# A norm five ticks later, later loads of mixed values, and weight splits in halves, in a one-core decoder layer

## The chip, the cores and the metric

The kernel runs on one core of a Trainium2 chip, as one launch. The metric is device time in microseconds (us); a kernel's time is the median of its runs. The profile shows one execution of the same program: which instruction ran on which engine, when, and what it waited for. The engines are named as in the profile: PE multiplies matrices (PEld is its weight load), DVE works on vectors, ACT evaluates functions and copies, POOL starts the adding transfers here, and SP starts the other transfers, one after the other.

## What is computed

One layer of a decoder trunk, for 2048 tokens of 1024 values. The part that matters here is the output projection and the norms around it:

```
mix = concatenate(gated DeltaNet output, HGRN2 output)       # 2048 x 1024
mix_out = mix @ w_out
h = x + rms_norm(mix_out, post_mix_norm)
u = rms_norm(h, pre_mlp_norm) @ w_mlp_up
y = square(relu(u)) @ w_mlp_down
h = h + rms_norm(y, post_mlp_norm)
e = rms_norm(p @ w_ple_proj, ple_norm)
h = h + e * sigmoid(h @ w_ple_gate)
rms_norm(x, w) = x * rsqrt(mean(x * x) + eps) * w
```

Ahead of it stand the input projection and the two mixers, which are chunked recurrences over the tokens. All is in 32-bit floats.

## The kernel before

Values are kept transposed: 128 of the 1024 features on the partitions, 512 tokens (a quarter) along the free axis. So a quarter of the activations is eight tiles of 128 x 512, and an output tile of `mix_out` is one tile of 128 x 512 made from eight tiles of mixed values. Each operand is split into a high part (ACT, a rounding copy) and a low part (DVE, value minus high part), and each product takes three matmuls (high by high, high by low, low by high). An output tile of `mix_out` is therefore 24 matmuls.

**The order of the work.** PE's instructions run in the order in which the program is written. For ACT, DVE and, in this stage, SP, a planner sets the order: it goes by the order in which instructions are written and by its own idea of when each could start. At run time each engine keeps that order strictly. To place the work beside the matmuls, the program has an agenda: `tick()` moves a clock on by one and issues the next step of every generator that is due. In the output projection `mm` calls `tick()` before every eighth matmul, so an output tile is three ticks. `later(gen, offsets)` puts the steps of a generator at these offsets from the current clock; `at(t, gen, offsets)` does so from a given clock.

**Two parts of the projection.** The last head of the last quarter still has a long tail of small dependent matmuls. The first seven output tiles (quarter 0, features 0 to 6) are computed between these (`early_outs`, lines 983 to 1010), eight matmuls to a tick. Then the main loop over `order` (lines 1384 to 1444) computes the other 25 tiles, 600 matmuls, in the order of `OUT_ORDER`: quarter 0's last tile, eight of quarter 1, then quarters 2 and 3 mixed. Below, "matmul 232" is the 232nd of these 600, counted from 0; the clock is 417 before the first, so the tick `c` comes before matmul 8 x (c - 417).

**The weights.** A block of `w_out` (128 x 1024 values) is fetched by `stage_out` into one of two buffers and split by `ready_out` into one of three. `OUT_ORDER` makes 19 such blocks. Blocks 0 to 7 are split in the tail, 8 to 18 in the main loop.

**The mixed values.** `mix_operands(q)` fetches and splits one of eight tiles at each step: a transfer of 256 KB, an ACT copy (line 225) and a DVE subtraction (line 226). Quarters 2 and 3 are placed by `later` at lines 1382 and 1383.

**The norms.** When a quarter of `mix_out` is done, `normed` runs (line 1435): `rstd_steps` splits the sum of squares into `hl` (first step), sums it over the partitions by two matmuls with a tile of ones and makes the reciprocal root on ACT and DVE (second step; tiles `nrm_o`, `r_o`). `residual_by_dma` then scales one of eight tiles a step (DVE, line 1235), adds the input `x` to it by an adding transfer started by POOL (line 1236), and five steps later squares the sum (ACT, line 241), adds it to a running total `acc_h` (DVE, line 242) and stores the tile (SP, line 1239, `h1d`). Last comes `rstd_steps` again on `acc_h`, two steps: the split `hl_h`, and the matmuls `nrm_h` with the chain that makes `rn`. `OUT_STEPS` holds the 17 offsets for quarter 0, `OUT_LAST` those for quarter 1. The tile `hl` has one buffer for all norms. Quarters 2 and 3 only get their `r_o` here (line 1440).

**What follows from the norms.** Once quarter 0's `rn` is issued, the next tile's start places `early_operands` (eight steps; each fetches a tile of `h1d`, scales it and splits it, tiles `be` and `t`). Once quarter 1's is issued, whatever is left of these runs at once and `rest_operands` follows. These tiles and the split blocks `w_u` feed the up projection, which begins after matmul 599.

Of the kernel before, what the change touches and what calls it, by code (L numbers as in the profile page):

```python
# [11 lines left out]
F32R = mybir.dt.float32r  # L12
# [8 lines left out]
P = 128  # L21
T = 2048
D = 1024
KD = D // P
# [22 lines left out]
OUT_ORDER = ("00 01 02 03 04 05 06 07 17 16 15 12 13 14 10 11 20 21 30 22 31 23 32 24 33 34 25 26 27 35 36 37")  # L47
SHARE = 6
TOGETHER = ((1, 7), (1, 6))
OUT_STEPS = (1, 5) + tuple(range(7, 20)) + (20, 26)  # L50
OUT_LAST = (1, 4) + tuple(range(5, 18)) + (19, 23)
MLP_STEPS = (1, 5) + tuple(range(7, 25, 2))
AMID_STEPS = (1, 5) + tuple(range(12, 39, 3))
# [43 lines left out]
def trunk(ctx, tc, x, xT, pT, vecs, w_in, w_ab, gdn_a_log, gdn_dt_bias, w_out, w_up, w_down,  # L97
          w_ple, w_gate, consts, out):
    nc = tc.nc
    V, S, G, PE = nc.vector, nc.scalar, nc.gpsimd, nc.tensor  # L100
# [4 lines left out]
    wp = wctx.enter_context(tc.tile_pool(name="wp", bufs=3, side="right"))  # L105
# [8 lines left out]
    def bank(name, pool=None):  # L114
        return (pool or pm).tile([P, QT], F32, tag="ps", name=name)

    def blk(c):
        return slice(c * P, (c + 1) * P)
# [51 lines left out]
    def split(t, eng, raw):  # L170

        S.activation(t[:, 0], raw, AF.Copy)  # L172
        eng.tensor_tensor(t[:, 1], raw, t[:, 0], ALU.subtract)  # L173
# [45 lines left out]
    def plain(t):  # L219

        return t[:, 1].bitcast(F32)

    def split_in_place(t):

        S.activation(t[:, 0], plain(t), AF.Copy)  # L225
        V.tensor_tensor(t[:, 1], plain(t), t[:, 0], ALU.subtract)  # L226
# [99 lines left out]
    def next_pool():  # L326
        turn[0] += 1
        return ra if (turn[0] - 1) % 28 < 10 else second[0]
# [3 lines left out]
    def mix_operands(q):  # L332
        xin[q] = []
        for k in range(KD):
            t = next_pool().tile([P, 2, QT], F32R, tag="ring", name=f"mixT{q}_{k}")
            nc.sync.dma_start(plain(t), mixd[q][k])
            split_in_place(t)
            xin[q].append(t)
            yield
# [11 lines left out]
    staged_out, ready = {}, {}  # L351

    def ready_at(n):
        return 0 if n < 3 else sorted(last_use[:n])[n - 3] + 1

    def stage_at(n):
        return 0 if n < 4 else ready_at(n - 2) + 1

    def stage_out(n):
        staged_out[n] = wp.tile([P, KD, P], F32, tag="raw", name=f"raw_out{n}", bufs=2)  # L360
        nc.sync.dma_start(staged_out[n], w_out[tile_of[n]])

    def ready_out(n):
        ready[n] = wp.tile([P, 2, KD, P], F32R, tag="whl", name=f"w_out{n}")
        split(ready[n], V, staged_out.pop(n))

    clock, agenda = [0], {}

# [81 lines left out]
    with mixers as mctx:  # L450
# [504 lines left out]
        def at(t, gen, offsets):  # L955
            for o in offsets:
                agenda.setdefault(t + o, []).append(gen)

        def call(t, fn):
            def once():  # L960
                fn()
                yield
            at(t, once(), (0,))
# [17 lines left out]
        last, end = t + LAST, SPT * len(works)  # L981
# [1 line left out]
        for n, o in enumerate((-12, -8, -4, 0, 4)):  # L983
            call(end + o, partial(stage_out, n))
        for n, o in enumerate((-6, -1, 3)):
            call(end + o, partial(ready_out, n))
        finished, held_y, square_sums = [], [], {q: None for q in range(NQ)}

        def early_outs():

            for j, (q, d) in enumerate(order):
                for n in range(3, len(tile_of)):
                    if ready_at(n) == j:
                        ready_out(n)
                for n in range(5, len(tile_of)):
                    if stage_at(n) == j:
                        stage_out(n)
                ps, w = bank(f"mmo_{q}_{d}"), ready[load_of[j]]
                for i in range(3 * KD):
                    k, term = i // 3, i % 3  # L1000
                    PE.matmul(ps, w[:, term // 2, k, :], xin[q][k][:, term % 2, :], start=i == 0, stop=i == 3 * KD - 1)  # L1001
                    if i % 4 == 3 and i + 1 < 3 * KD:
                        yield
                        while i > KD and held_y:
                            nc.sync.dma_start(*held_y.pop())
                y = m2.tile([P, QT], F32, tag="ld", name=f"yo{q}_{d}", bufs=2)
                S.activation(y, ps, AF.Copy)
                square_sums[q] = squares(square_sums[q], ps, d, f"o{q}")
                finished.append(j)
                held_y.append((yod[q][d], y))  # L1010
                yield
# [129 lines left out]
    def later(gen, offsets):  # L1141
        for o in offsets:
            agenda.setdefault(clock[0] + o, []).append(gen)
# [21 lines left out]
    def ytile(name):  # L1165
        return f2.tile([P, QT], F32, tag="y", name=name, bufs=16)
# [103 lines left out]
    def run(gen):  # L1270
        for _ in gen:
            pass
# [95 lines left out]
    def two_blocks(*them):  # L1368

        w = wp.tile([P, 2, KD, P], F32R, tag="whl", name=f"w_u{them[0][0]}")  # L1370
        halves = [w[:, :, : KD // 2], w[:, :, KD // 2 :]]
        for t, it in zip(halves, them):
            if it:
                u_block(it[0], t, it[1])
        return halves[1]

    pair[0] = True
    early = None
    made, held = {q: [None] * KD for q in range(NQ)}, {}
    mix1 = mix_operands(1)  # L1380
    run(mix1)
    later(mix_operands(2), range(5, 21, 2))
    later(mix_operands(3), range(12, 28, 2))
    for j, (q, d) in enumerate(order):
        if j in finished:
            made[q][d] = ytile(f"yo{q}_{d}")
            nc.sync.dma_start(made[q][d], yod[q][d])
            continue
        for n in range(2, len(tile_of)):
            if ready_at(n) == j:  # L1390
                ready_out(n)
        for n in range(3, len(tile_of)):
            if stage_at(n) == j:
                stage_out(n)
        if j == len(order) - 5:
            u_raw = [wp.tile([P, 2, QT], F32, tag="raw", name=f"u_raw{i}", bufs=2) for i in range(2)]
            a1, a2 = w_up[0], w_up[FF // P // 2]
            for t, i, src in ((u_raw[0], 0, a1[:, : KD // 2]), (u_raw[1], 1, a1[:, KD // 2 :]),
                              (u_raw[0], 1, a2[:, : KD // 2]), (u_raw[1], 0, a2[:, KD // 2 :])):
                nc.sync.dma_start(t[:, i].rearrange("p (k n) -> p k n", n=P), src)  # L1400
        if j == len(order) - 2:
            two_blocks(("11", u_raw[0][:, 0]), ("12", u_raw[1][:, 1]))
        if j == len(order) - 1:
            (a11, a21), (s1, s4) = ((t[:, 0], t[:, 1]) for t in u_raw)
            b22 = two_blocks(("22", s1), None)
            V.tensor_tensor(s1, s1, a21, ALU.add)
            V.tensor_tensor(a21, a11, a21, ALU.subtract)
            V.tensor_tensor(a11, s1, a11, ALU.subtract)
            V.tensor_tensor(s4, s4, a11, ALU.subtract)
            u_block("3", b22, a21)  # L1410
            later(prep, range(3 * KD // 2))
        if early is None and h1_r[0] is not None:
            early = early_operands()
            later(early, range(0, 2 * KD, 2))
        if prep is None and h1_r[1] is not None:
            run(early)
            prep = rest_operands(h1_r[1])
            later(prep, range(3 * KD // 2))
        if j in held:
            ps = held.pop(j)  # L1420
        elif order[j] == TOGETHER[0]:
            held = {j + i: bank(f"mmo_{q}_{d}_{i}", pp) for i in range(len(TOGETHER))}
            sides = [columns(ready[load_of[i]]) for i in held]
            for k in range(KD):
                for i, w in zip(held, sides):
                    product(held[i], w[k : k + 1], xin[q][k : k + 1], k == 0, k == KD - 1)
            ps = held.pop(j)
        else:
            ps = bank(f"mmo_{q}_{d}", pp)
            product(ps, columns(ready[load_of[j]]), xin[q])  # L1430
        y = ytile(f"yo{q}_{d}") if q < 2 else tp.tile([P, QT], F32, tag="stg", name=f"yo{q}_{d}")
        S.activation(y, ps, AF.Copy)
        acc = square_sums[q] = squares(square_sums[q], ps, d, f"o{q}")
        made[q][d] = y
        if q >= 2:
            nc.sync.dma_start(yod[q][d], y)
        if all(of != q for of, _ in order[j + 1 :]) and q < 2:
            later(normed(q, made[q], acc, lambda d, q=q: xT[blk(d), tok(q)], R_POSTMIX, h1d[q], "o", "h"),
                  OUT_LAST if q else OUT_STEPS)
        elif all(of != q for of, _ in order[j + 1 :]):  # L1440
            later(rstd_steps(acc, 1.0 / D, EPS, f"o{q}", row_of(o_r, q), po, wait=True),
                  OUT_STEPS[:2] + (9,) if q == 2 else (12, 20, 24))
    u_block("2", two_blocks(("1", s1), None), a11)
    u_block("4", wp.tile([P, 2, KD // 2, P], F32R, tag="raw", name="w_u4", bufs=2), s4)
    run(prep)
# [468 lines left out]
```

## Time and profile before

| | us |
|---|---|
| median of 3 runs | 2713.89 (2713.32 to 2715.02) |
| the profiled execution's own time | 2702.87 |
| its span, first to last instruction | 2701.1 |
| PE busy | 2652.0 (98%) |
| DVE busy | 2031.1 (75%) |
| ACT busy | 1458.9 (54%) |
| POOL busy | 137.0 (5%) |
| tail with the first seven output tiles | about 1061.7 to 1121.4 |
| main loop of the output projection | 1121.4 to 1271.0 |

A row of the timeline gives an instruction's start, its duration, engine, line, operation, and output and input tiles; in brackets the idle time of the engine just before it and what ended that. Consecutive like instructions are merged into one row with a count. A row of the waits reads: who waited, for what, total us, times, longest. PE's matmuls overlap in the pipeline, so one is listed with 0.39 us while in a long row they follow one another at less than that.

### The profile page before, as it was taken

Reading aid. Unit: us, or ns where it says so; the run is one execution under the profiler, and the core shown is the slowest. Engines: PE = TensorE matmul, PEld = TensorE weight load, DVE = VectorE, ACT = ScalarE, POOL = GpSimd, SP = SyncE. Lnnn points to the kernel's source line nnn. Section 1 sums busy time; section 2 is a strip of 40 time slices with the busy share of each in tenths; the row PEclk is TensorE's granted clock in tenths of the full one; section 3 lists DMA queues with packets and bytes.
Section 4 is the critical chain, followed back from the end, with each engine's and each line's share of the span. In section 5 each row is a group of like instructions: output and inputs, shape, how many; then the busy total and the mean of one; then the engine's idle time right before and its main releaser. Section 6 shows DMA issues by size and latency. Waiting matters only on the chain.

```text
span 2701.1 us, 38432 instructions
## 1 busy us (share of the span) xinstructions
PE 2652.0 (98%) x12745; PEld 2210.0 (82%) x12745; DVE 2031.1 (75%) x4200; ACT 1458.9 (54%) x2935; POOL 137.0 (5%) x147
## 2 busy tenths in 40 slices
PE   8999999999999999999999999999999999999999
PEld 6788888888888887878888878888888888888887
DVE  7778878787778777578989867768877765468775
ACT  7665655465446445566556555554555555565431
POOL 0000000000000000020000000001000001101000
PEclk9999999999999999999999999999999999999999
DMA  8777777667666665584656466666544465577663
GB/s 278 275 242 247 239 250 248 224 222 249 209 211 219 211 212 187 181 224 153 210 205 213 172 223 218 210 201 236 191 160 145 165 225 185 201 249 247 216 215 125
DMA packets 267766, 573.51 MB, mean 212 GB/s; under 512 B 55578, under 2 KB 60152, under 8 KB 250416
## 3 DMA queue, kind: packets, MB, share of 16 engines
q1 hardware_dynamic: 265264, 566.86, 61.9%
q0 software_dynamic: 2304, 4.20, 0.9%
q8 instruction: 101, 1.65, 0.3%
q14 instruction: 97, 0.79, 0.1%
HBM read 410.57 MB, written 160.37 MB: 211 GB/s over the span
## 4 chain that ended last, share of the span: by engine, by line
PE 50%; issue 4%; DVE 3%; DMA 3%; ACT 2%; POOL 1%; SPq 0%; DVEq 0%; ACTq 0%; POOLq 0%
PE u L1150 22%; PE d L1150 19%; PE mmg L1150 6%; DMA dr<-in_w_down_dram 1%; PE mme L199 1%; PE mmo L1150 1%; PE mmo L1001 0%; POOL acc_y L242 0%; DMA h1d<-yo 0%; DMA sys_g<-ud_g 0%; DMA yo<-in_xT_dram 0%; DVE w_out L173 0%; DMA rd_g<-m_g 0%; DMA db<-hid 0%; DVE b L1306 0%
## 5 line engine op out<-in xcount | busy, mean ns | idle before, releaser
L1118 PE MATMUL mm<-xt,w 128*128 128x512 f32 x3072 | 783.9, 400 | 1.9 <-ACT zt_zg L592 1.3
L1118 PEld LDWEIGHTS mm<-xt,w 128*128 128x128 f32 x3072 | 553.4, 189 | 102.7 <-ACT zt_zg L592 1.7
L1150 PE MATMUL d<-db,da 128*128 128x512 f32 x2688 | 614.5, 389 | 2.0 <-ACT db L225 1.5
L1150 PEld LDWEIGHTS d<-db,da 128*128 128x128 f32 x2688 | 504.4, 188 | 108.4 <-ACT db L225 2.3
L1150 PE MATMUL u<-t,wu 128*128 128x512 f32 x2604 | 591.3, 389 | 0.0
L1150 PEld LDWEIGHTS u<-t,wu 128*128 128x128 f32 x2604 | 488.8, 188 | 101.5
L226 DVE TENSOR_TENSOR db<-db 128x512 fp32r<-128x512 f32 x224 | 161.1, 719 | 51.6 <-ACT db L225 50.6
L1537 DVE TENSOR_TENSOR u<-u,u 128x512 f32<-128x512 f32 x224 | 150.4, 683 | 57.3 <-PE u L1150 55.9
L1150 PE MATMUL mmg<-h2T,wg 128*128 128x512 f32 (+1 forms) x792 | 174.8, 383 | 0.0
L225 ACT ACTIVATE db<-db 128x512 fp32r<-128x512 f32 x224 | 140.9, 629 | 59.4 <-DMA db<-hid 55.4
L1580 ACT ACTIVATE u<-u 128x512 f32<-128x512 f32 x128 | 80.8, 631 | 164.3 <-DVE u L1537 163.6
L1150 PEld LDWEIGHTS mmg<-h2T,wg 128*128 128x128 f32 x792 | 145.6, 188 | 29.1
L173 DVE TENSOR_TENSOR da<-da 128x512 fp32r<-128x512 f32 x128 | 94.7, 740 | 77.6 <-ACT da L172 77.3
L1150 PE MATMUL mmo<-mixT,w_out 128*128 128x512 f32 x600 | 139.2, 393 | 0.3 <-DVE w_out L173 0.3
L172 ACT ACTIVATE da<-da 128x512 fp32r<-128x512 f32 x128 | 80.5, 629 | 108.8 <-DMA da<-sumd 82.0
L1150 PEld LDWEIGHTS mmo<-mixT,w_out 128*128 128x128 f32 x600 | 114.0, 190 | 24.5 <-DVE w_out L173 0.8
L173 DVE TENSOR_TENSOR da<-dr,da 128x512 fp32r<-128x512 f32 x96 | 68.9, 718 | 43.5 <-ACT da L172 41.8
L172 ACT ACTIVATE wu<-a 128x512 fp32r<-128x512 f32 x124 | 75.1, 623 | 44.6 <-DMA a<-in_w_up_dram 40.8
L713 DVE TENSOR_TENSOR pr_g<-xs_g,sys_g 128x16 f32<-128x16 f32 (+14 forms) x240 | 94.5, 394 | 5.7
L173 DVE TENSOR_TENSOR wu<-a,wu 128x512 fp32r<-128x512 f32 x124 | 85.7, 693 | 10.4 <-ACT wu L172 10.3
L1581 ACT ACTIVATE u<-u 128x512 f32<-128x512 f32 x128 | 80.5, 629 | 3.1
L172 ACT ACTIVATE da<-dr 128x512 fp32r<-128x512 f32 x96 | 60.5, 631 | 33.2 <-DMA dr<-in_w_down_dram 28.6
(390 smaller groups left out, 3821.3 us busy)
## 6 DMA issues: line engine op xcount, KB each, us to landing
w<-cache_in SPq DMA_DIRECT2D x96, 1024.0 KB
db<-hid SPq DMA_DIRECT2D x224, 256.0 KB
cache_in<-w SPq DMA_DIRECT2D x32, 1024.0 KB
hid<-u SPq DMA_DIRECT2D x128, 256.0 KB
da<-sumd SPq DMA_DIRECT2D x128, 256.0 KB
a<-in_w_up_dram SPq DMA_DIRECT2D x124, 256.0 KB
hid<-ht SPq DMA_DIRECT2D x96, 256.0 KB
dr<-in_w_down_dram SPq DMA_DIRECT2D x96, 256.0 KB
```

The costliest lines, as they stand in the source:

```text
L172: S.activation(t[:, 0], raw, AF.Copy)
L173: eng.tensor_tensor(t[:, 1], raw, t[:, 0], ALU.subtract)
L199: PE.matmul(ps, a, b, start=i == 0, stop=i == n - 1)
L225: S.activation(t[:, 0], plain(t), AF.Copy)
L226: V.tensor_tensor(t[:, 1], plain(t), t[:, 0], ALU.subtract)
L713: V.tensor_tensor(pr[:, :, :, 0:i], xs[:, None, :, 0:i].broadcast_to([P, 2, GC, i]), sys[:, 0:i, i : i + 2].rearrange("p j two -> p two j" ...
L1118: PE.matmul(ps, *terms[i], start=i == 0, stop=i == nt - 1)
L1150: PE.matmul(ps, a, b, start=start, stop=stop)
L1537: V.tensor_tensor(c[new], c[old], ps, ALU.add)
L1580: S.activation(c[k], c[k], AF.Relu)
L1581: S.activation(c[k], c[k], AF.Square)
```

## The change

Five things, all in or near the output projection:

- The last two offsets of `OUT_STEPS` go from 20 and 26 to 29 and 31: quarter 0's `hl_h` is split nine ticks later, and its norm (`nrm_h`, `rn`) follows five ticks later.
- `mix_operands` of quarters 2 and 3 starts three ticks later (8 and 15 instead of 5 and 12), with the same spacing.
- `early_operands` gets six places, two ticks apart, instead of eight; what is left of it runs when quarter 1's `rn` has been issued.
- Quarter 2's `r_o` is made at the offsets 8, 13 and 17 instead of 1, 5 and 9.
- The `w_out` blocks that are made ready in the tail (0 to 7) are split by a new generator in two halves, a tick apart, placed on the agenda.

```diff
-OUT_STEPS = (1, 5) + tuple(range(7, 20)) + (20, 26)
+OUT_STEPS = (1, 5) + tuple(range(7, 20)) + (29, 31)
...
+    def ready_halves(n):
+        ready[n] = wp.tile([P, 2, KD, P], F32R, tag="whl", name=f"w_out{n}")
+        raw = staged_out.pop(n)
+        for sl in (slice(0, KD // 2), slice(KD // 2, KD)):
+            split(ready[n][:, :, sl], V, raw[:, sl])
+            yield
...
         for n, o in enumerate((-6, -1, 3)):
-            call(end + o, partial(ready_out, n))
+            at(end + o, ready_halves(n), (0, 1))
...
                     if ready_at(n) == j:
-                        ready_out(n)
+                        at(clock[0], ready_halves(n), (0, 1))
...
-    later(mix_operands(2), range(5, 21, 2))
-    later(mix_operands(3), range(12, 28, 2))
+    later(mix_operands(2), range(8, 24, 2))
+    later(mix_operands(3), range(15, 31, 2))
...
             early = early_operands()
-            later(early, range(0, 2 * KD, 2))
+            later(early, range(0, 12, 2))
...
             later(rstd_steps(acc, 1.0 / D, EPS, f"o{q}", row_of(o_r, q), po, wait=True),
-                  OUT_STEPS[:2] + (9,) if q == 2 else (12, 20, 24))
+                  (8, 13, 17) if q == 2 else (12, 20, 24))
```

## The prediction, made before the result was known

> **What bounds the kernel now.** I read the page first (where PE loses time), then the waits of PE in the tail and in the main loop, then PE's timeline around the longest wait, and last the timelines of ACT, DVE and SP at that place.
>
> ```profile
> span 2701.1 us, 38432 instructions
> PE 2652.0 (98%) x12745; PEld 2210.0 (82%) x12745; DVE 2031.1 (75%) x4200; ACT 1458.9 (54%) x2935; POOL 137.0 (5%) x147
> ```
>
> PE is the bound; only its idle or slow time can be won. The waits of PE, tail first, then from 1121 us on:
>
> ```profile
> PE at_h L868 <- ACT keys_h L873: 2.1, 1, 2.1
> PE psb_g L784 <- DVE r_g L781: 1.4, 2, 0.9
> ...
> PE nrm_h L1181 <- ACT hl_h L172: 5.7, 1, 5.7
> PE u L1150 <- DVE w_u L173: 0.4, 1, 0.4
> ...
> PE u L1150 <- ACT w_u L172: 0.3, 1, 0.3
> ```
>
> The 5.7 us belong to quarter 0's second norm. PE's timeline, two rows of the tail and then there:
>
> ```profile
> 1075.93 0.71 PE L868 MATMUL at_h<-qk_h,keys_h 128*128 128x128 f32 x4 [2.05 <-ACT keys_h L873]
> 1076.40 1.17 PE L1001 MATMUL mmo<-mixT,w_out 128*128 128x512 f32 x4
> ...
> 1167.77 8.91 PE L1150 MATMUL mmo<-mixT,w_out 128*128 128x512 f32 x38 [0.33 <-DVE w_out L173]
> 1182.33 0.79 PE L1181 MATMUL nrm_h<-hl_h,ones 128*128 128x512 f32 x1 [5.66 <-ACT hl_h L172]
> 1183.48 0.79 PE L1182 MATMUL nrm_h<-hl_h,ones 128*128 128x512 f32 x1 [0.35 <-DVE hl_h L173]
> 1184.07 5.52 PE L1150 MATMUL mmo<-mixT,w_out 128*128 128x512 f32 x16
> 1189.43 0.39 PE L1181 MATMUL nrm_o<-hl_o,ones 128*128 128x512 f32 x1
> ...
> 1189.88 34.62 PE L1150 MATMUL mmo<-mixT,w_out 128*128 128x512 f32 x152
> 1224.33 0.39 PE L1181 MATMUL nrm_h<-hl_h,ones 128*128 128x512 f32 x1
> 1224.81 0.50 PE L1182 MATMUL nrm_h<-hl_h,ones 128*128 128x512 f32 x1
> ```
>
> A matmul costs 34.62 / 152 = 0.228 us, an undisturbed pair of norm matmuls 1189.88 - 1189.43 = 0.45. PE was at the norm at 1182.33 - 5.66 = 1176.67. Undisturbed it would have reached `nrm_o` of quarter 1 after the pair and 16 matmuls, at 1176.67 + 0.45 + 3.64 = 1180.76; it got there at 1189.43. So this place costs **8.7 us**: 6.0 idle (5.66 + 0.35), and 2.7 in which matmuls ran slowly: the 16 took 1189.43 - 1184.07 = 5.36 instead of 3.64, and the pair 1.0 too long. The granted clock, the third number from the end of that window's row, fell below full there:
>
> ```profile
> 1180.00:1200.00 20.00, 17.32 (x65) 13.82 (x66) 14.19 (x24) 16.23 (x24) 0.62 (x1) 0.83 0.44 157
> ```
>
> Why `hl_h` was late: ACT, DVE, SP (first two ACT rows: the tail).
>
> ```profile
> 1074.52 1.06 ACT L172 ACTIVATE w_out<-raw_out 128x1024 fp32r<-128x1024 f32 x1 [3.48 <-DMA raw_out<-in_w_out_dram]
> 1075.48 0.40 ACT L873 ACTIVATE keys_h<-qk_h 128x256 f32<-128x256 f32 x1
> ...
> 1165.05 0.62 ACT L225 ACTIVATE mixT<-mixT 128x512 fp32r<-128x512 f32 x1
> ...
> 1173.96 1.06 ACT L172 ACTIVATE w_out<-raw_out 128x1024 fp32r<-128x1024 f32 x1 [6.04 <-DMA raw_out<-in_w_out_dram]
> ...
> 1181.65 0.63 ACT L172 ACTIVATE hl_h<-acc_h 128x512 fp32r<-128x512 f32 x1 [0.61 <-DVE acc_h L242]
> ...
> 1184.31 0.63 ACT L172 ACTIVATE hl_o<-acc_o 128x512 fp32r<-128x512 f32 x1 [1.06 <-PE nrm_h L1182]
> 1184.96 1.28 ACT L1186 ACT_TABLE_LOAD   x1
> ```
> ```profile
> 1175.57 0.69 DVE L242 TENSOR_TENSOR acc_h<-acc_h,sq_h 128x512 f32<-128x512 f32 x1 [7.25 <-ACT sq_h L241]
> ...
> 1182.13 0.69 DVE L226 TENSOR_TENSOR mixT<-mixT 128x512 fp32r<-128x512 f32 x1
> 1182.73 0.69 DVE L173 TENSOR_TENSOR hl_h<-acc_h,hl_h 128x512 fp32r<-128x512 f32 x1
> 1183.34 0.69 DVE L242 TENSOR_TENSOR acc_o<-acc_o,sq_o 128x512 f32<-128x512 f32 x1
> ```
> ```profile
> 1153.36 0.86 SPq L336 DMA_DIRECT2D mixT<-mixd  x2
> 1160.80 3.49 SPq L1239 DMA_DIRECT2D h1d<-yo  x3
> 1164.39 1.23 SPq L361 DMA_DIRECT2D raw_out<-in_w_out_dram  x1
> 1165.71 6.38 SPq L1239 DMA_DIRECT2D h1d<-yo  x4
> ...
> 1174.14 0.32 SPq L1239 DMA_DIRECT2D h1d<-yo  x1
> ```
>
> ACT stood 6.04 us at the split of `w_out` block 13, whose transfer, started at 1164.39 behind three stores, landed only at 1173.96, 9.6 us later. Everything behind it on ACT waited, DVE with it, and then DVE worked without a gap from 1175.57 to 1184.03. The block itself is used from matmul 288 on: the split is early, the squares behind it are not.
>
> **Quarter 0's norm.** The matmuls go from matmul 232 to 272, the split from tick 440 to 449. Nothing is removed: one split (0.63 ACT, 0.69 DVE), two matmuls (0.45), the chain of `rn` with two table loads of 1.28; it issues no transfer, so SP and POOL are not passed. The 8.7 us at matmul 232 go. But ACT's block at 1173.96 stays, and the next thing due is now `nrm_o` of quarter 1, at matmul 248, whose `hl_o` stands in the same queue. PE reaches it at 1176.67 + 3.64 = 1180.3. The last `acc_o` that it needs ended at 1184.03. Ahead of it `hl_h` leaves (0.60, from 1182.73 to 1183.34), and so does the last `mixT` (0.60, from 1182.13), which is now issued at tick 446, behind the split of `hl_o` at 445: 1182.8. `hl_h` let PE go 1182.33 - 1181.65 = 0.68 after ACT began it; so 1183.5, and PE stands 3.2 us, and 0.35 more for the low part. Bounds: nothing, if the planner puts the total's last terms ahead of the mixed values; 5.0 + 0.35, if no slot but `hl_h`'s leaves and two more `mixT` come in. For the slow clock: the wait of 2.05 in the tail was followed by no slow matmul (the row behind it has four in 1.17, where 0.39 + 3 x 0.228 = 1.07 is undisturbed), the one of 6.0 by 2.7 us. In line between them 3.55 idle costs 2.7 x (3.55 - 2.05) / (6.0 - 2.05) = 1.0. So 3.2 + 0.35 + 1.0 = 4.6 of the 8.7 come back; **net -4.1**, bounds -8.7 and -1.1 (5.35 idle, and the 2.3 us that fit it). `hl` has one buffer, so `hl_h` follows `nrm_o`; PE is 24 matmuls (5.5 us) away then, against 0.63 + 0.69: covered by 4 us.
>
> **Mixed values.** Sixteen steps, each a transfer of 256 KB on SP, 0.62 ACT and 0.69 DVE, three ticks (24 matmuls, 5.5 us) later. Needed: quarter 2's last tile at matmul 237, quarter 3's at 285. Issued now at ticks 439 and 446, matmuls 176 and 232: 61 and 53 matmuls, 13.9 and 12.1 us, ahead. So they cost nothing as long as the queues keep within 12 us; how late ACT and DVE run there is the 6 to 7 us of the block. On SP the last two loads stood at 1153.36, just before the first `h1d` store, which had to wait until 1160.80. Three ticks later they can fall behind it: a rival. They free ACT and DVE before 1167, where PE waited 0.33 for `w_out`: I take **-0.3** (0 to -0.33).
>
> **Early operands and quarter 2's norm.** `rn` comes five ticks later, and so do the eight pieces; two of them now run after quarter 1's norm (matmul 408), each 0.75 + 0.69 of DVE. DVE is full there:
>
> ```profile
> 1240.00:1260.00 20.00, 20.00 (x90) 16.57 (x89) 18.43 (x28) 8.09 (x15) 0.00 (x0) 1.00 0.46 158
> 1266.72 1.28 ACT L1186 ACT_TABLE_LOAD   x1
> ```
>
> So 2.9 us of DVE come in; against them quarter 2's chain leaves the stretch before the up projection: two table loads and three short ACT operations (2 x 1.28 + 3 x 0.63 = 4.5 us of ACT) and about as many on DVE (5 x 0.65 = 3.2). The 0.3 and 0.4 us that PE waited for `w_u` lay right behind that chain: **-0.7**, bounds 0 and +2.2 if only the 2.9 show. Quarter 1's second norm had no slack (0.48 from its first matmul to the second at 1224.81, where half of 0.45 is due); its chain starts with `nrm_o` and no longer has quarter 0's Ln and Exp ahead of it. Nothing taken.
>
> **Halves.** Eight splits become sixteen instructions on each of ACT and DVE. By the 128x512 rows a half costs 0.63 and 0.69, the whole:
>
> ```profile
> L172 ACT ACTIVATE w_out<-raw_out x19: 1042/1061/1069, 1045.2 to 1240.4; 128x1024 fp32r<-128x1024 f32 x19
> L173 DVE TENSOR_TENSOR w_out<-raw_out,w_out x19: 1210/1221/1226, 1050.0 to 1243.7; 128x1024 fp32r<-128x1024 f32 x19
> ```
>
> That is 0.2 ACT and 0.16 DVE more for each block, 3 us in all, beside PE in the tail. PE's 2.05 us at 1075.93 came from `keys_h` standing behind a block whose transfer was late (3.48). A half first lets it go 0.43 earlier; if block 2, which has long arrived, goes first, all 2.05 go. Against it, a second half can fall before an `r_g` (0.69). I take **-1.2**, bounds +0.7 and -2.05.
>
> **Sum.** 4.1 + 0.3 + 0.7 + 1.2 = 6.3 us less. Against the profiled execution, 2702.87 - 6.3 = 2696.6; the median of the runs shown stands 2713.89 - 2702.87 = 11.0 above that, so **2707.6** is forecast (-0.23%).
>
> **The rivals.** First, no wait takes its place: the total's terms come out ahead of `mixT` and of the block's split on DVE. 8.7 + 0.3 + 0.7 + 2.05 = 11.8 us less, 2702.1. For it: the rows from 1175.57 to 1184.03 hold some 14 slots of 0.6, and `hl_o` does not need them all. Against it: DVE is 7.25 us behind at their start whatever the order. Second, the slow clock comes in full after 3.55 us of idle as it did after 6.0: 2.7 instead of 1.0 us, 1.7 more than forecast, 2709.3; the rows, harmless at 2.05 and full at 6.0, leave it open. [...] Third, the wait only moves on: 5.35 idle and 2.7 slow, and the planner fills the tail as before; 0.65 + 0.4 less, 2712.8. For it: `hl_o` was released by nothing but the same late queue. That the planner leaves ACT and DVE in their old order, so that the later issue changes nothing but PE, belongs here. Fourth, slower: the last mixed values' loads fall behind the last `h1d` store (1174.14) and take as long as block 13 (9.6 us), and ACT stands there to 1183.7 instead of 1173.96. Then `hl_o` is 9.7 later still: 13.3 idle and 2.7 slow, 16.0 against 8.7, so +7.3 less the 2.2 elsewhere: 2719.0. With half that delay it is 2714.2. It decides from a release at about 1177 on, where the new wait eats the 8.7. For it: the transfer engines (second number from the end, a share) were nearly full when these would run. Against it: in the 20 us before they had a quarter free, and the last two loads, at 1153.36, were 14 to 18 us ahead of their places (matmuls 192 and 208, with 194 at 1167.77).
>
> ```profile
> 1140.00:1160.00 20.00, 20.00 (x90) 16.56 (x89) 15.64 (x23) 17.63 (x28) 5.34 (x6) 1.00 0.74 231
> 1160.00:1180.00 20.00, 16.34 (x71) 12.88 (x69) 12.23 (x19) 9.78 (x16) 2.91 (x4) 1.00 0.91 243
> ```
>
> **Chances.** Forecast 0.27 (2704 to 2710), no new wait 0.20, slow clock in full 0.14, moved on 0.20, slower case 0.19. What a measurement of this kernel can tell from no change is about 0.2%, 5.4 us: faster is below 2708.5. That is three quarters of the forecast, all of the first rival, a third of the second and little of the third: 0.47. Slower is above 2719.3: most of the last, since other late pieces would add to it, 0.17. The rest is 0.36. The range, 2700 to 2720, takes in the first rival and the slower case up to a little above its price.
>
> **What would show it.** Right: the wait of `nrm_h` is gone at matmul 272 and 3 to 4 us stand at `nrm_o` of quarter 1 instead; ACT's 6 us at the split of block 13 are still there; the wait of `at_h` is shorter than 2.05. Wrong: a wait of `mmo` for `mixT`, ACT waiting for a `mixT` transfer beyond 1174, `nrm_h` of quarter 1 or `u` waiting for microseconds, or a clock below 1.00 in a stretch where it was full.

## The result and the profile after

The changed kernel takes 2707.74 us in the median (2705.07 to 2712.42, 13 runs), the kernel before 2713.60 (2710.64 to 2717.29, 13 runs). The ratio is 0.9979, 95% interval 0.9971 to 0.9988: 5.7 us less, between 3.3 and 7.9. The forecast was 2707.6.

The two profiled executions don't show this as they stand: the one of after took 2706.48 us (span 2704.7), the one of before 2702.87. The difference arises ahead of the change. The first output tile of the tail begins at 1061.70 in the one and 1067.18 in the other, and over the 14 profiles of this study it begins anywhere from 1059.76 to 1068.92, though the program up to there differs only in a few splits. From the first `wu` matmul of the up projection to the end all 14 agree within 2.3 us (1409.27 to 1411.57). So kernels are compared by stages, between four instructions that each of them has on PE: T, the first output tile in the tail; A, the first matmul of the main loop; B, `nrm_o` of quarter 1 (behind matmul 247); C, the first matmul of `u` with `wu`. A second profile of the changed kernel is in the table too. A single profile is a coarse measure: the two profiles of each of three kernels (the changed one, and the two with block 13 held below) differ by 1.3 to 1.9 us in A to C, so a difference of that size between two kernels is not shown by this column alone.

| kernel | T to A | A to B | B to C | A to C |
|---|---|---|---|---|
| before | 59.75 | 67.98 | 101.82 | 169.80 |
| after, first profile | 59.33 | 66.09 | 101.33 | 167.42 |
| after, second profile | 61.82 | 63.77 | 102.25 | 166.02 |

PE's timeline of after, from the matmuls behind quarter 0's `nrm_o` on (start, duration, engine, line, operation, tiles, count, and in brackets the idle time before and its releaser; lines past the new function are seven higher than before):

```profile
1143.26 29.63 PE L1157 MATMUL mmo<-mixT,w_out 128*128 128x512 f32 x130
1175.04 11.91 PE L1157 MATMUL mmo<-mixT,w_out 128*128 128x512 f32 x44 [2.15 <-DVE w_out L173]
1188.92 3.72 PE L1157 MATMUL mmo<-mixT,w_out 128*128 128x512 f32 x10 [1.97 <-DVE mixT L226]
1192.60 0.80 PE L1188 MATMUL nrm_o<-hl_o,ones 128*128 128x512 f32 x1
1193.32 0.54 PE L1189 MATMUL nrm_o<-hl_o,ones 128*128 128x512 f32 x1
1193.70 5.64 PE L1157 MATMUL mmo<-mixT,w_out 128*128 128x512 f32 x24
1199.18 0.39 PE L1188 MATMUL nrm_h<-hl_h,ones 128*128 128x512 f32 x1
```

The stall of `nrm_h` is gone, at matmul 232 and at its new place. Two others stand there: 2.15 us for `w_out` block 12 at matmul 194, and 1.97 us for `mixT`, the last tile of quarter 2, at matmul 238. Matmuls behind both are slow (the granted clock was 0.50 there, last section): 44 took 11.91 us where 44 x 0.228 = 10.03 is undisturbed, ten took 1192.60 - 1188.92 = 3.68 instead of 2.28, the norm's pair 1.10 instead of 0.45. In all 2.15 + 1.88 + 1.97 + 1.40 + 0.65 = 8.0 us, against 8.7 + 0.33 before.

ACT and DVE at that place:

```profile
1168.07 0.63 ACT L234 ACTIVATE acc_h<-yo 128x512 f32<-128x512 f32 x1 [4.19 <-DMA yo<-in_xT_dram]
...
1169.09 1.05 ACT L172 ACTIVATE w_out<-raw_out 128x1024 fp32r<-128x1024 f32 x1
...
1180.61 1.06 ACT L172 ACTIVATE w_out<-raw_out 128x1024 fp32r<-128x1024 f32 x1 [5.60 <-DMA raw_out<-in_w_out_dram]
```
```profile
1182.23 0.69 DVE L242 TENSOR_TENSOR acc_h<-acc_h,sq_h 128x512 f32<-128x512 f32 x1 [6.64 <-ACT sq_h L241]
...
1185.84 1.22 DVE L173 TENSOR_TENSOR w_out<-raw_out,w_out 128x1024 fp32r<-128x1024 f32 x1
...
1188.18 0.69 DVE L226 TENSOR_TENSOR mixT<-mixT 128x512 fp32r<-128x512 f32 x1
```

ACT still stands 5.60 us at the split of block 13. Quarter 2's last `mixT` now stands behind that block's split on DVE (1188.18 and 1185.84), and PE needs it at 1186.95. With the old offsets it stood ahead of the split. The rows carry no tile numbers, but the kernel with the norm's move alone (below) shows it: PE passed this matmul at about 1182.1 there without a wait, and the block's split came only at 1183.39. The wait for block 12 has another source: its split stands behind `acc_h` on ACT, which waited 4.19 us (before: 1.24) for the first adding transfer.

In PE's timeline of the second profile of after, `w_out` is not waited for (ACT's wait for the first adding transfer is 2.08) and `mixT` for 3.18 us:

```profile
1183.42 0.96 PE L1157 MATMUL mmo<-mixT,w_out 128*128 128x512 f32 x3 [0.17 <-DVE mixT L226]
1187.57 3.92 PE L1157 MATMUL mmo<-mixT,w_out 128*128 128x512 f32 x10 [3.18 <-DVE mixT L226]
1191.33 0.42 PE L1188 MATMUL nrm_o<-hl_o,ones 128*128 128x512 f32 x1
```

There the place costs 0.17 + 3.18 and 2.3 of slow matmuls, 5.6 us.

### The profile page after: what moved, and what is told of

The parts are those of the page before. It is cut to its first block, busy times and chain, and to the rows that moved or that the text cites. A ratio compares the mean times of both kernels' runs of the same rounds, so it can differ in the third digit from the quotient of the medians.

```text
span 2704.7 us, 38442 instructions
## 1 busy us (share of the span) xinstructions
PE 2654.4 (98%) x12745; PEld 2209.5 (82%) x12745; DVE 2030.6 (75%) x4208; ACT 1457.8 (54%) x2943; POOL 137.4 (5%) x147
## 4 chain that ended last, share of the span: by engine, by line
PE 53%; DMA 4%; DVE 2%; issue 1%; ACT 1%; POOL 1%; SPq 0%; POOLq 0%; DVEq 0%; ACTq 0%
PE u L1157 22%; PE d L1157 20%; PE mmg L1157 6%; PE mmo L1157 3%; DMA dr<-in_w_down_dram 1%; PE mme L199 1%; POOL acc_y L242 1%; DMA raw_out<-in_w_out_dram 1%; DMA rsb_g<-rd_g 0%; PE mmo L1008 0%; DMA rd_g<-m_g 0%; ACT sq_y L241 0%; DMA yo<-in_xT_dram 0%; DMA mixT<-mixd 0%; ACT da L172 0%
## 5 line engine op out<-in xcount | busy, mean ns | idle before, releaser
L173 DVE TENSOR_TENSOR wu<-a,wu 128x512 fp32r<-128x512 f32 x124 | 85.7, 693 | 12.0 <-ACT wu L172 11.9
```

## Experiments

Theories. *Moved wait*: the root of the stall is block 13's late transfer, which holds ACT; the norm's new place leaves that alone, and the next product that PE needs is late instead. *Mixed values*: the new waits come from the later loads of mixed values, and without these the norm's move would win all. *Elsewhere*: the gain comes from the halves or from quarter 2's norm. The stages of all kernels, and the ratio of each one's time to that of the kernel before, run beside it:

| kernel | T to A | A to B | B to C | A to C | ratio (95%) |
|---|---|---|---|---|---|
| norm alone | 61.48 | 64.43 | 104.77 | 169.20 | 0.9986 (0.9976 to 0.9996) |
| mixed values alone | 61.44 | 69.24 | 103.03 | 172.27 | 1.0008 (1.0000 to 1.0017) |
| halves alone | 61.77 | 67.99 | 103.00 | 170.99 | 0.9998 (0.9988 to 1.0007) |
| early and quarter 2 alone | 61.94 | 68.22 | 100.21 | 168.43 | 0.9992 (0.9983 to 1.0001) |
| after without the norm's move | 61.85 | 68.95 | 100.18 | 169.13 | 0.9994 (0.9985 to 1.0002) |
| after, mixed values at old offsets | 60.38 | 62.77 | 103.87 | 166.64 | 0.9967 (0.9956 to 0.9978) |
| before, block 13 held | 60.09 | 60.55 | 108.62 | 169.17 | 0.9991 (0.9982 to 1.0000) |
| after, block 13 held | 59.40 | 59.20 | 105.01 | 164.21 | 0.9958 (0.9945 to 0.9970) |
| the same again | 61.51 | 58.50 | 103.80 | 162.30 | 0.9964 (0.9950 to 0.9978) |
| that, mixed values at old offsets | 62.19 | 58.55 | 103.48 | 162.03 | 0.9967 (0.9955 to 0.9980) |
| the same again | 62.27 | 58.04 | 102.73 | 160.77 | 0.9956 (0.9943 to 0.9968) |

0.001 is 2.7 us. A to B undisturbed is 248 x 0.228 = 56.5 and two or three pairs of norm matmuls at 0.45 (one of `nrm_g`, one of quarter 0's `nrm_o`, and `nrm_h` where it is early): 57.4 to 57.9.

**The norm alone.**

```diff
-OUT_STEPS = (1, 5) + tuple(range(7, 20)) + (20, 26)
+OUT_STEPS = (1, 5) + tuple(range(7, 20)) + (29, 31)
```

> The kernel before with only the offsets 29 and 31 of quarter 0's norm. Moved-wait theory (ACT is held by the late transfer of w_out block 13 whatever the tick of the norm, and the next product that PE needs is late instead): no wait of nrm_h at matmul 232, and 3 to 4 us of PE at nrm_o of quarter 1, since the last acc_o behind the block ended at 1184.03 and PE gets there at 1180.3; ACT still stands 5 to 6 us at the split of block 13. Time 4 to 5 us under the kernel before. Mixed-values theory (the two new waits of the changed kernel, 2.15 us for w_out and 1.97 us for mixT, come from the later loads of mixed values, and nothing else replaces the stall): none of the three waits, and 8 to 9 us under the kernel before. Elsewhere theory (the gain of the changed kernel comes from the halves and quarter 2's norm): within 1 us of the kernel before.

PE's timeline of this kernel at the place:

```profile
1172.09 12.53 PE L1150 MATMUL mmo<-mixT,w_out 128*128 128x512 f32 x54 [1.38 <-DVE w_out L173]
1188.93 0.79 PE L1181 MATMUL nrm_o<-hl_o,ones 128*128 128x512 f32 x1 [4.31 <-ACT hl_o L172]
1189.66 0.79 PE L1182 MATMUL nrm_o<-hl_o,ones 128*128 128x512 f32 x1
1190.25 7.49 PE L1150 MATMUL mmo<-mixT,w_out 128*128 128x512 f32 x24
1197.58 0.39 PE L1181 MATMUL nrm_h<-hl_h,ones 128*128 128x512 f32 x1
```

The wait moved where the prediction put it: 4.31 us at `nrm_o` of quarter 1; ACT stood 6.24 us at block 13. Behind it the pair and 24 matmuls took 1197.58 - 1188.93 = 8.65 us instead of 5.92: 2.7 us of slow clock (0.50 from 1187.33 to 1194.15). With the 1.38 for `w_out` the place costs 8.4 us, and A to C falls by 0.6 only. By the runs it is 3.8 us (1.1 to 6.5), near the 4 to 5 that were expected; the stages do not show where the rest came from. Mixed values as the sole cause is out: they stood at their old offsets here.

**The mixed values alone**, later, and **the changed kernel with them at the old offsets**.

```diff
-    later(mix_operands(2), range(5, 21, 2))
-    later(mix_operands(3), range(12, 28, 2))
+    later(mix_operands(2), range(8, 24, 2))
+    later(mix_operands(3), range(15, 31, 2))
```

> The kernel before with only the mixed values of quarters 2 and 3 three ticks later. Moved-wait theory: the wait of nrm_h at matmul 232 stays at 5 to 7 us, since block 13 still holds ACT; nothing else changes by more than 1 us, so the time is within 1 us of the kernel before. Mixed-values theory: ACT's wait for the first added yo grows from 1.24 to about 4.2 us as in the changed kernel, w_out of block 12 comes late and PE waits about 2 us for it at matmul 194, and mixT of quarter 2's last tile about 2 us at matmul 237, ahead of or in place of a part of the nrm_h wait: 2 to 6 us over the kernel before.

PE's timeline of the mixed values alone:

```profile
1189.36 0.79 PE L1181 MATMUL nrm_h<-hl_h,ones 128*128 128x512 f32 x1 [7.78 <-ACT hl_h L172]
```

No new wait in the stretch, but the old one is longer (7.78 against 5.66), and it ends later: 62.9 us behind A, before 60.9. ACT waited 2.73 us for the first adding transfer. That wait is 1.19 to 1.85 us in the eight profiles with the old offsets and 2.08 to 4.19 in the six with the later ones, so the later loads do delay this transfer. What that costs is less certain: 2.5 us in A to C against before, 1.3 against the halves alone, whose main loop is that of before, and 2.2 (0 to 4.6) by the runs. The expected wait at matmul 194 did not show.

> The changed kernel with the mixed values at their old offsets, all else as changed. Moved-wait theory: the waits for w_out (2.15) and mixT (1.97) go, but 3 to 4 us at nrm_o of quarter 1 take their place (plus the slow matmuls behind), so that the time is within 2 us of the changed kernel's. Mixed-values theory: both waits go and nothing replaces them: 7 to 8 us under the changed kernel, some 13 under the kernel before.

PE's timeline of the changed kernel with the old offsets:

```profile
1174.49 12.57 PE L1157 MATMUL mmo<-mixT,w_out 128*128 128x512 f32 x54 [0.61 <-DVE w_out L173]
1190.48 0.80 PE L1188 MATMUL nrm_o<-hl_o,ones 128*128 128x512 f32 x1 [3.41 <-ACT hl_o L172]
1191.20 0.79 PE L1189 MATMUL nrm_o<-hl_o,ones 128*128 128x512 f32 x1
1191.79 7.97 PE L1157 MATMUL mmo<-mixT,w_out 128*128 128x512 f32 x24
1199.60 0.39 PE L1188 MATMUL nrm_h<-hl_h,ones 128*128 128x512 f32 x1
```

The waits for `w_out` and `mixT` shrink to 0.61 and nothing, and 3.41 us stand at `nrm_o`, with 9.12 - 5.92 = 3.2 us of slow clock behind. 7.2 us in this place, against 8.0 and 5.6 with the later loads: the same loss at another product. By the runs it is 8.9 us under the kernel before (6.0 to 11.9), where the changed kernel is 5.7 (3.3 to 7.9); the intervals overlap.

**Block 13 held back.** In the kernel before and in the changed one its load and split were put behind output tile 15. The loads of blocks 14 and 15 move behind it. The planner moves a load ahead whenever its buffer is free, so a copy of four columns into the buffer makes it wait:

```diff
-    def stage_out(n):
+    def stage_out(n, after=None):
         staged_out[n] = wp.tile([P, KD, P], F32, tag="raw", name=f"raw_out{n}", bufs=2)
+        if after is not None:
+            V.tensor_copy(staged_out[n][:, 0, :4], after[:, :4])
...
-            if ready_at(n) == j:
+            if {13: 17}.get(n, ready_at(n)) == j:
...
-            if stage_at(n) == j:
-                stage_out(n)
+            if {13: 16, 14: 17, 15: 18}.get(n, stage_at(n)) == j:
+                stage_out(n, y if n == 13 else None)
```

> The changed kernel with the load and the split of w_out block 13 held back until output tile 15 of the order is done (a copy of four columns of that tile into the buffer ahead of the load makes the load wait), which puts the load behind all h1d stores of quarter 0 on SP and the split behind hl_o on ACT. If block 13's late transfer is the cause of the wait for mixT (moved-wait theory): ACT's 5.6 us at that split go, the wait of 1.97 us at matmul 238 and the slow matmuls behind it go (1.97 + 1.3 + 0.65), the wait for w_out of block 12 (2.15) stays: 3 to 4 us under the changed kernel. If the mixed values' later loads are the cause: the wait for mixT stays, and the time is that of the changed kernel. If block 13 now comes too late for its own first use at matmul 288, a new wait for w_out shows there.

PE's and ACT's timelines of the changed kernel with the block held:

```profile
1175.06 12.54 PE L1159 MATMUL mmo<-mixT,w_out 128*128 128x512 f32 x54 [0.60 <-DVE w_out L173]
1187.52 0.49 PE L1190 MATMUL nrm_o<-hl_o,ones 128*128 128x512 f32 x1
1188.24 0.50 PE L1191 MATMUL nrm_o<-hl_o,ones 128*128 128x512 f32 x1 [0.23 <-DVE hl_o L173]
```
```profile
1186.83 0.63 ACT L172 ACTIVATE hl_o<-acc_o 128x512 fp32r<-128x512 f32 x1 [2.10 <-DVE acc_o L242]
1190.24 1.06 ACT L172 ACTIVATE w_out<-raw_out 128x1024 fp32r<-128x1024 f32 x1 [2.78 <-DMA raw_out<-in_w_out_dram]
```

The wait for `mixT` is gone though the mixed values are as late as in after; no slow clock shows in the main loop (the 24 matmuls behind the norm's pair took 1194.04 - 1188.58 = 5.46 us, 0.228 each), and A to B is 59.20. Issued at 1186.23, behind the stores, the block lands in 4.0 us instead of the 9.6 of the kernel before. So the block at its old place was the cause of `mixT`'s wait. The edit moves the block's load and its split together: how much of the wait was ACT's standing for the transfer (5.60 us) and how much the split's own place ahead of `mixT` on DVE (1.22 us), it does not tell apart. Expected were 3 to 4 us under the changed kernel; by the two ratios it is 5.7, and the wait for block 12, expected to stay, was 0.60.

> The kernel before (quarter 0's norm still at matmul 232) with the load and the split of w_out block 13 held back until output tile 15 of the order is done, as in the run with the changed kernel. If block 13's late transfer is the root of the stall: ACT's 6.0 us at that split are gone from the stretch ahead of the norm, and of the 5.7 us of nrm_h at matmul 232 only 1 to 2 us stay, since in the changed kernel with block 13 held back the last total of quarter 0's squares ended at 1184.3, about 1 us after PE passed the place of matmul 232; with 2 us or less and no slow clock 5 to 8 us go: the block's delay alone gains as much as the whole change, or more. If the late squares come from the adding transfers or from DVE instead: the wait stays at 4 us or more and the time within 2 us of the kernel before.

PE's timeline of the kernel before with the block held:

```profile
1181.71 0.50 PE L1183 MATMUL nrm_h<-hl_h,ones 128*128 128x512 f32 x1 [0.65 <-ACT hl_h L172]
...
1186.85 30.99 PE L1152 MATMUL mmo<-mixT,w_out 128*128 128x512 f32 x136
1220.59 0.73 PE L1152 MATMUL mmo<-mixT,w_out 128*128 128x512 f32 x2 [2.75 <-ACT w_out L172]
1222.22 5.07 PE L1152 MATMUL mmo<-mixT,w_out 128*128 128x512 f32 x14 [0.89 <-DVE w_out L173]
```

ACT and SP ahead of the wait at 1220.59:

```profile
1214.82 0.63 ACT L241 ACTIVATE sq_h<-yo 128x512 f32<-128x512 f32 x1 [2.81 <-DMA yo<-in_xT_dram]
...
1219.48 1.06 ACT L172 ACTIVATE w_out<-raw_out 128x1024 fp32r<-128x1024 f32 x1
```
```profile
1190.01 0.37 SPq L363 DMA_DIRECT2D raw_out<-in_w_out_dram  x1
```

The norm's stall, at its old place, falls from 5.66 to 0.65 us and A to B by 7.4 us: the block was the root there too. But PE then waits 2.75 + 0.89 us at matmul 384 for block 15, with a period of half clock behind (0.51 from 1222.50 to 1225.92), and 1.6 us for `w_u` later; B to C is 6.8 us longer, and 2.4 us (0 to 4.9) are left by the runs. Block 15 takes block 13's buffer, but its transfer is not what was late: it left SP at 1190.01, and ACT did not wait for it at 1219.48. Its split stood in ACT's queue behind quarter 1's squares, for whose adding transfers ACT waited, the last time 2.81 us. It came 93.6 us behind A, in the kernel before 95.2 (1216.64 - 1121.45); PE, freed of the stall, got to matmul 384 at 1217.84, 92.0 behind A, where it had passed there 99.4 behind A. So the wait moved on once more, to the next product that ACT held. In the changed kernel, with the same hold, ACT waited 1.34 us at most for these transfers, and PE 0.82 for block 15. The expectation of 5 to 8 us was wrong about that.

> The changed kernel with both: mixed values at their old offsets and block 13 held back. If the wait at nrm_o (3.4 us, with the clock at half for 6.8 us behind it, in the run with the mixed values at their old offsets) is the block's doing: it goes, and the time is 5 to 7 us under that run, about 2699. If the mixed values' later loads cost something by themselves, beyond the place where the stall comes up, this kernel is also 1 to 2 us under the changed kernel with block 13 alone held back (2700.75); if they don't, the two agree within 1 us.

> The changed kernel with block 13 held back, again, beside the next one on one chip. No wait of 1.5 us or more in the main loop and no half clock there; 6 to 12 us under the kernel before. If the later mixed loads cost nothing once the stall is gone, the next kernel agrees with it within 1.5 us.

> The same with the mixed values at their old offsets. If the later mixed loads delay the first adding transfer by themselves (ACT waited 1.2 to 1.9 us for it with the old offsets and 2.1 to 4.2 us with the later ones) but PE has slack for that, the two kernels agree within 1.5 us; if not, this one is 2 us or more the faster.

With the mixed values at their old offsets as well no wait above 0.6 us is left in the main loop. The waits of PE there in the second of the two runs (who, for what, total us, times, longest):

```profile
PE nrm_h L1191 <- DVE hl_h L173: 0.4, 1, 0.4
PE nrm_g L280 <- DVE hl_g L173: 0.4, 1, 0.4
PE mmo L1159 <- DVE w_out L173: 0.3, 1, 0.3
```

A to B is 58.55 and 58.04, close to what PE's own work takes. The second run with the block alone held came out as expected: no wait above 0.89 us and no half clock in the main loop. Both versions are faster than the kernel before: 11.4 and 9.7 us with the block held, 8.9 and 11.9 with the mixed values at the old offsets too (intervals from 5.4 to 15.4). All four are above the 5.7 us of the changed kernel, but some intervals overlap with its 3.3 to 7.9. Between the two versions the runs do not decide; A to C is 1.5 to 2.2 us shorter with the old offsets, about as much as two profiles of one kernel differ. Against the changed kernel with the old offsets and the block not held, 5 to 7 us less were expected: A to C is 4.6 to 5.9 less, but by the runs one ratio is the same (8.9 and 8.9) and one 3.0 us lower.

**The norm's move taken out of the change.** The opposite of the first diff, on the changed kernel.

> The changed kernel with quarter 0's norm back at the offsets 20 and 26, all else as changed. If the norm's place is what lets the other edits pay (moved-wait theory): the wait of nrm_h at matmul 232 is back with 6 to 8 us, as in the run with the mixed values alone (7.8), and the main loop takes to quarter 1's nrm_o 68 to 70 us instead of 64 to 66; the time is 5 to 8 us over the changed kernel, level with the kernel before or 2 us above it. If the other edits carry the gain: within 2 us of the changed kernel.

PE's timeline of that kernel:

```profile
1183.64 0.79 PE L1188 MATMUL nrm_h<-hl_h,ones 128*128 128x512 f32 x1 [7.58 <-ACT hl_h L172]
```

The stall is back, 7.58 us, A to B 68.95, and the time is 1.6 us under the kernel before (from 4.1 under to 0.5 over). By the ratios that is 4.1 us over the changed kernel, a little less than the 5 to 8 expected. The norm's move is what wins in A to B, and the later mixed values lengthen the stall when it stays.

**Halves alone**: only the generator `ready_halves` and its two calls.

> The kernel before with only the splits of w_out blocks 0 to 7 in halves. Moved-wait theory: the wait of at_h falls from 2.1 to about 1.6 us, the stall of nrm_h at matmul 232 stays at 5 to 8 us with its slow clock, and the time is 0 to 1.5 us under the kernel before. Elsewhere theory (the halves carry the gain): 3 us or more under the kernel before, and most of it lies between the first output tile in the tail and the main loop.

PE's timeline of the halves alone, in the tail and at the stall:

```profile
1076.80 1.22 PE L875 MATMUL at_h<-qk_h,keys_h 128*128 128x128 f32 x4 [2.59 <-ACT keys_h L880]
...
1184.92 0.79 PE L1188 MATMUL nrm_h<-hl_h,ones 128*128 128x512 f32 x1 [5.59 <-ACT hl_h L172]
```

Nothing is won. The wait of `at_h` is 2.05, 2.21, 2.17, 2.62 and 2.37 us in the five profiles with whole splits, and 1.62, 1.70, 2.25 and 2.53 to 2.97 in the nine with halves. The wait for `r_g` ahead of it, which the prediction named as a danger, rose from 0.90 to 0.91 us in the five to 1.46 to 1.51 in the nine, while one of 0.35 to 0.38 for `S_g` went. The ratio is 0.9998.

**Early operands and quarter 2's norm alone.**

```diff
-            later(early, range(0, 2 * KD, 2))
+            later(early, range(0, 12, 2))
...
-                  OUT_STEPS[:2] + (9,) if q == 2 else (12, 20, 24))
+                  (8, 13, 17) if q == 2 else (12, 20, 24))
```

> The kernel before with only the six places of the early operands and quarter 2's norm at 8, 13 and 17. By the prediction's step PE's waits for w_u (0.3 and 0.4 us) at the start of the up projection go, 0.7 us or less, and the stall of nrm_h stays at 5.5 to 6 us: within 1 us of the kernel before. If two of the early pieces now crowd DVE ahead of the up projection, up to 2.2 us over it, with a wait of u for t.

PE's timeline of that kernel, from quarter 1's second norm into the up projection:

```profile
1227.12 0.40 PE L1181 MATMUL nrm_h<-hl_h,ones 128*128 128x512 f32 x1
...
1227.59 45.51 PE L1150 MATMUL mmo<-mixT,w_out 128*128 128x512 f32 x200
1272.94 7.42 PE L1150 MATMUL u<-t,w_u 128*128 128x512 f32 x32
```

PE no longer waits for `w_u`. The 84 matmuls of `u` up to C take 1292.43 - 1272.94 - 0.45 (the norm's pair, which now lies among them) = 19.04 us, before 1291.25 - 1270.95 = 20.30; quarter 1's `nrm_h` pair takes 0.47 instead of 0.82. Together 1.6 us, which is B to C's difference; in the changed kernel without the norm's move, which has these two edits, B to C is as short (100.18). No wait of `u` for `t` shows. By the runs it is 2.2 us under the kernel before (4.6 under to 0.3 over), which is not clear of nothing.

**The second profile of after**, told above.

> The changed kernel once more, for a second profile of it. If the two waits (w_out of block 12, mixT of quarter 2's last tile) belong to the program and not to one execution, both are there again with 1.5 to 3 us each, and the clock falls to half for about 3.4 us behind each that fills more than half of one of its periods of 3.4 us.

This came true in half: `mixT` is again waited for, with one period of half clock behind (0.50 from 1187.10 to 1190.51); `w_out` is not, so that wait belongs to the one execution. What was expected of the clock was the author's estimate; it fits the first profile, where PE was idle for 60 and 58% of the 3.41 us ahead of each fall (last section).

## Why the prediction was right in its number, and where it was not

**The norm.** The mechanism is shown: ACT's block stays, and the wait of `nrm_h` moves to `nrm_o` of quarter 1. Forecast were 3.2 + 0.35 us there, measured 4.31 (the norm alone) and 3.41 (with all but the mixed values). The term that was mis-sized is the slow clock behind it: 1.0 taken, 2.7 and 3.2 measured. That is the second rival's mechanism. The step took the harmless 2.05 us in the tail as a lower end of length and drew a line from there; it was the place of that wait in time (last section). So the norm alone, forecast at -4.1, is worth -0.6 in A to C against before and -1.8 against the halves alone, whose main loop is the same; added to the early operands and quarter 2's norm it is -1.8 too (168.43 to 166.64). By the runs it is -3.8 (-1.1 to -6.5), in which the forecast lies too, so that the size of this term rests on the profiles.

**The mixed values.** The step failed: taken at -0.3, "they cost nothing as long as the queues keep within 12 us". Alone they cost 1.3 to 2.5 us (A to C) or 2.2 (0 to 4.6, by the runs). With block 13 held A to C is 1.5 to 2.2 us longer with them, which the runs do not confirm. The mechanism is plainer than the size. On DVE the planner put quarter 2's last tile behind block 13's split, so that in after the wait stood at `mixT` and never got as far as `nrm_o`. The sign named as "wrong", a wait of `mmo` for `mixT`, is there. The fourth rival is not its reason: the last two loads left SP at 1159.59, ahead of the first `h1d` at 1168.07, and ACT did not wait for them.

**Early operands and quarter 2's norm.** Right in kind; -0.7 taken from the two printed waits, -1.6 measured, because PE lost more around them than the waits (1276.81 - 1270.95 - 24 x 0.228 = 0.39 and 1277.95 - 1276.81 - 2 x 0.228 = 0.68, with 0.25 and 0.41 listed as waits) and the pair of `nrm_h`, "nothing taken", counted as well; this is a figure of profiles, and the runs leave it between 4.6 less and 0.3 more.

**Halves.** Failed: -1.2 taken, nothing measured. The wait of `at_h` stayed; the one for `r_g` grew by 0.6 us, where one of 0.4 for `S_g` went.

**The sum.** In the stretch of the stall 9.0 us became 8.0 in one execution and 5.6 in the other, where 4.4 less was forecast for the norm and the mixed values; with 1.6 of the early operands this makes 2.6 to 5.0 us less, where the runs say 3.3 to 7.9. The forecast of 6.3 less lies in the runs' interval, but its terms did not come out so: the norm's and the halves' gains were put too high, the mixed values' cost was missed, and quarter 2's gain was put too low. That 2707.6 met 2707.74 is luck. What the runs show beyond the stages is not explained; two profiles of after, 1.4 us apart in A to C, can't settle it. Of the rivals, the wait that only moves on is nearest to what the stretch shows in the first profile, though its time (2712.8, 1.1 us less) lies outside what the runs say; "no wait takes its place" is out for this change; only holding block 13 made it so.

## What to carry to other kernels

When a product is late because an engine stands at something else in its queue, moving the consumer hands the wait to the next consumer; look for what the engine stands at and move that. Here the load that blocked ACT was wanted 56 matmuls after the stall, and holding it back took 7.4 us out of the stretch where the five edits together took 1.9 and 4.2. Then look for the next product in that queue: in the kernel before with the block held, PE came 7.4 us earlier to block 15, whose split ACT made only 1.6 us earlier, and most of the gain was given back there and behind it. And price a stall with the clock behind it: here waits of 1.97 and 2.15 us cost 4.0 each.

## What the runs showed of the hardware

In these traces the granted clock fell and recovered on a grid of 3.41 us; the waits ahead of the falls in the tail and the main loop were 1.97 to 7.78 us long. Windows of after, laid on the falls and recoveries (window, its length, busy time and count of PE, PEld, DVE, ACT, POOL, then the granted clock, the share of the transfer engines, GB/s):

```profile
1172.98:1176.40 3.42, 1.36 (x6) 1.14 (x7) 2.61 (x4) 1.11 (x2) 0.83 (x1) 1.00 1.10 276
1176.40:1179.81 3.41, 3.41 (x10) 2.63 (x9) 0.00 (x0) 0.00 (x0) 0.00 (x0) 0.50 1.07 320
...
1186.62:1190.03 3.41, 1.44 (x7) 0.93 (x6) 3.41 (x7) 1.58 (x3) 0.00 (x0) 1.00 0.55 158
1190.03:1193.44 3.41, 3.41 (x9) 1.91 (x7) 2.54 (x5) 1.52 (x3) 0.00 (x0) 0.50 0.98 327
```

The falls, at 1176.40 and 1190.03, are 13.63 = 4 x 3.41 us apart, and each lasts 3.41. Falls farther apart keep the step: 19.27 and 1176.40 in after are 339 x 3.413 us apart, 20.37 and 1180.90 in before 340 x 3.413, 1081.29 and 1187.10 in the second profile of after 31 x 3.413. The period ahead of the two falls above had PE busy for 1.36 and 1.44 us, 40 and 42%. The two periods of half clock list 10 and 9 matmuls, the full one behind the first (1179.81 to 1183.22) lists 17: about half the work, by this grid an estimated 1.7 us lost; 1.88 and 1.40 + 0.65 were read above. The run with the mixed values at the old offsets shows two such periods in a row (PE was busy for 2.92 of 3.41 in the first of them), and a tail wait of 2.68 us with no half clock behind it, in a period with PE busy to 50%. Both from windows of that kernel:

```profile
1186.57:1189.99 3.42, 0.50 (x3) 0.07 (x1) 3.19 (x6) 1.77 (x4) 0.00 (x0) 1.00 0.80 247
1189.99:1193.40 3.41, 2.92 (x6) 2.10 (x7) 2.05 (x3) 2.76 (x5) 0.00 (x0) 0.50 0.91 311
1193.40:1196.81 3.41, 3.41 (x9) 2.64 (x9) 0.00 (x0) 3.34 (x5) 0.00 (x0) 0.50 0.75 287
```
```profile
1080.77:1084.18 3.41, 1.70 (x11) 1.53 (x12) 2.02 (x4) 1.86 (x4) 0.00 (x0) 1.00 0.68 187
1084.18:1087.59 3.41, 3.41 (x25) 3.07 (x24) 2.80 (x10) 1.98 (x8) 1.11 (x1) 1.00 0.16 56
```

In the second profile of after a shorter wait of `at_h`, 2.53 us, fell into one period, and the next is at half (0.52, since the window's edges are 0.1 us off the grid):

```profile
1077.76:1081.18 3.42, 0.89 (x5) 0.46 (x5) 1.50 (x5) 1.42 (x3) 0.00 (x0) 1.00 0.42 112
1081.18:1084.59 3.41, 3.41 (x12) 2.83 (x11) 2.93 (x9) 1.23 (x4) 0.84 (x1) 0.52 0.43 143
```

So what a wait of about 2 us cost here went with its place on the grid, a matter of luck. The 2.05 us of before, on which the prediction built, lay across a boundary, at 1075.12: PE was busy for 2.17 and 2.60 us of the two periods, and no half clock followed. Busy shares close to one another went with different clocks, though: in the second profile of after a half period busy to 2.94 of 3.41 (at 1187.10) was followed by full clock, where the one busy to 2.92, above, was followed by another at half. Of the 14 profiles nine had a half period in the tail between 1060 and 1097, with T to A 61.44 to 62.27, and five had none there, 59.33 to 60.38: about 2 us apart, and the changed kernel's own two profiles stand one on each side. The kernel before is among the five.
